# A hybrid decoder step on one core: in the Mamba stage, ScalarE and an adding transfer make every third block's second part, and ScalarE takes the convolution's first tap

## The chip, the cores and the metric

The kernel runs on one core of a Trainium2 chip. The metric is the device time of one execution in microseconds (us), smaller is better. The core's engines work side by side, each in the order of its own instructions: TensorE (PE in the rows; PEld is its loading of weights), VectorE (DVE), ScalarE (ACT), GpSimd (POOL) and SyncE (SP, which here only issues transfers). SBUF is the memory on the chip that they share; PSUM is the small memory into which TensorE writes.

## The reference

One inference step of a trunk of two layers, in fp32, for a prompt of 512 positions and a sample group of 8 x 8, which share the weights. The even layer is windowed attention beside an S5 state space model, the odd layer is a Mamba-2 mixer, and each is followed by an MLP. The change lies in the odd layer:

```python
def _mamba2(h, conv_buf, ssm_h0, w_in, conv_w, conv_b, dt_bias, a_log, d_skip, gnorm_w, w_out):
    zxbcdt = h @ w_in
    z, xbc, dt = ...
    xbc_full = jnp.concatenate([left, xbc], axis=1)
    conv = lax.conv_general_dilated(xbc_full, conv_w[:, None, :].astype(xbc.dtype), ...)   # 4 taps, causal, per channel
    xbc_c = jax.nn.silu(conv.astype(f32) + conv_b.astype(f32))
    x, bm, cm = ...
    dt = jax.nn.softplus(dt.astype(f32) + dt_bias.astype(f32)).reshape(bsz, l, G_C, J_C)
    y, h_last = _ssd(x * dt[..., None], dt * a, bm, cm, h0, chunk)
    ...
    g = (y * jax.nn.silu(z.astype(f32)))
    g = g * lax.rsqrt(jnp.mean(g * g, axis=-1, keepdims=True) + RMS_EPS)
    out = g.astype(h.dtype) @ w_out
```

## The kernel before

All 576 positions (512 + 64) lie along the free dimension, in two halves of 288 (`HV`), and the channels lie on the 128 partitions. A matrix product in fp32 is made of three products of parts: a weight block `w` of 128x1024 (8 pieces of 128x128) is split into a first part `wh`, which is `w` rounded to the form that TensorE multiplies, and a second part `wl` = `w` − `wh`; the activations are split in the same way into `xh` and `xl`. TensorE adds `wh`·`xh`, `wh`·`xl` and `wl`·`xh` (L326, L347 and L348 for the input projection, L1289 to L1291 for the output projection), over 8 pieces and two halves: 48 matmuls for a block.

`split_block` (L302) makes the parts. SP loads the raw block of 512 KB into a ring of two buffers (`NW` = 2). ScalarE copies it to `wh` (`copy_a`, L290). Then L312 subtracts on VectorE, or, for every third block (`SHARE_ODD` = 3, counted in `self.blocks`), on GpSimd. `wh` and `wl` have two buffers each in this stage. A raw buffer is free again, and the next load into it can start, when both parts have been made.

`odd` (L1108) is the Mamba stage, about 780 to 1345 us of the profiled execution. Its projection has 41 blocks: z (blocks 0 to 15), x (16 to 31), B (32 to 35), C (36 to 39) and dt (40). The blocks of x, B and C go through `raw_evac` (L1150ff), where ScalarE copies the result from PSUM to a tile `raw`, half by half, and GpSimd copies its last columns to `cvo`. Then `conv_tile` (L1138) follows: the first tap with the bias gives `cacc` on GpSimd (L1141), taps two to four are added on VectorE (L1143), ScalarE takes the tanh `cth` (L287), and VectorE multiplies it with `cacc` to x, B or C (L1146, L1148). There are 24 such tiles of 128x600. `dt_post` makes from dt what the state space scan needs, among it `tq` (L1238 to L1242 on VectorE), which TensorE transposes (L1247). `ssd_group` computes the scan for a group of heads, `gate` and `gated_norm` follow, then `out_proj`.

Two things set the order of work. The string `ODD_ORDER` gives the order in which the program names its parts: `s` a piece of the scan, `b`, `x` and `z` a part of the projection, `a`, `g` and `o` gate, norm and output projection. A scheduler then sets the order of instructions on each engine from that program and from modelled times; so an instruction that moves to another engine can move others too. An engine then runs its instructions strictly in that order.

Of the kernel before, what the change touches and what calls it, by code (L numbers as in the profile page):

```python
# [9 lines left out]
F32 = mybir.dt.float32  # L10
F32R = mybir.dt.float32r
ACTF = mybir.ActivationFunctionType
ALU = mybir.AluOpType
# [204 lines left out]
class _Kernel:  # L218
# [83 lines left out]
    def split_block(self, src, ring=None, cuts=1):  # L302

        raw = self.block(src, (8, 128), ring, cuts)
        hi, lo = self.part_tiles()
        self.blocks += 1
        eng = self.nc.gpsimd if self.share and self.blocks % self.share == 0 else self.nc.vector
        n = 8 // cuts
        for i in range(cuts):
            f = lambda t: t[:, i * n:i * n + n].rearrange("p a b -> p (a b)")  # L310
            self.copy_a(f(hi), f(raw))
            eng.tensor_tensor(f(lo), f(raw), f(hi).bitcast(F32), ALU.subtract)  # L312
        return hi, lo

    def pin(self, place):
# [796 lines left out]
    def odd(self, h, spill, done):  # L1112
        nc, tc, a = self.nc, self.tc, self.a
        tt, v = nc.vector.tensor_tensor, nc.vector
        stt = nc.vector.scalar_tensor_tensor
        with ExitStack() as es:
# [13 lines left out]
            cw = od.tile([128, 120], F32, name="cw")  # L1130
# [7 lines left out]
            def conv_tile(m, raw, out):  # L1138

                acc = od.tile([128, 600], F32, tag="cv", name=self.nm("cacc"), bufs=NCV)  # L1140
                nc.gpsimd.tensor_scalar(acc, raw[:, 0:600], cw[:, 4 * m:4 * m + 1], cw[:, 96 + m:97 + m], ALU.mult, ALU.add)  # L1141
                for k in range(1, 4):
                    stt(acc, raw[:, k:k + 600], cw[:, 4 * m + k:4 * m + k + 1], acc, op0=ALU.mult, op1=ALU.add)  # L1143
                th = od.tile([128, 600], F32, tag="cv", name=self.nm("cth"), bufs=NCV)
                self.act(th, acc, ACTF.Tanh)
                stt(out[:, 0:SEQ], th[:, 0:SEQ], 1.0, acc[:, 0:SEQ], op0=ALU.add, op1=ALU.mult)  # L1146
                s_in = lambda t: t[:, 512:600].rearrange("p (b k) -> p b k", b=8)[:, :, 3:11]
                stt(out[:, SEQ:].rearrange("p (b t) -> p b t", b=8), s_in(th), 1.0, s_in(acc), op0=ALU.add, op1=ALU.mult)  # L1148
# [19 lines left out]
            def evac(mt, hf, ps):  # L1168
                sl = slice(*HV[hf])
                if mt == 40:  # L1170

                    v.tensor_scalar(dtr[:, sl], ps[:96], po[:96, 696:697], None, ALU.add)
                    return
                if mt < 16:

                    if mt not in zs:
                        zs[mt] = ol.tile([128, T], F32, tag="z", name=self.nm("z"), bufs=4)
                    th = od.tile([128, HALF], F32, tag="cv", name=self.nm("zth"), bufs=NCV)
                    self.act(th, ps, ACTF.Tanh, scale=0.5)
                    stt(zs[mt][:, sl], th, 1.0, ps, op0=ALU.add, op1=ALU.mult)  # L1180
                    return
                m = mt - 16
                if not raw_evac(m, hf, ps):
                    return
                raw = raws.pop(m)
                if m < 16:
                    xs[m] = ol.tile([128, T], F32, tag="xs", name=self.nm("xs"), bufs=NXS)
                    conv_tile(m, raw, xs[m])
                else:
                    key = ("B" if m < 20 else "C", (m - 16) % 4)  # L1190
                    bc[key] = od.tile([128, T], F32, tag=key[0], name=self.nm(key[0]), bufs=2)
                    conv_tile(m, raw, bc[key])
# [78 lines left out]
            m = self.halves(self.mring)  # L1271
# [415 lines left out]
```

## Time and profile before

| | |
|---|---|
| median of 3 executions | 1770.38 us (1768.38 to 1774.1) |
| the profiled execution, its own time | 1776.06 us |
| its span, from the first instruction to the last | 1773.9 us |
| mean granted clock of TensorE | 0.967 of full speed |
| busy: TensorE | 1665.1 us (94%) |
| busy: VectorE | 1190.5 us (67%) |
| busy: ScalarE | 770.9 us (43%) |
| busy: GpSimd | 670.4 us (38%) |

The busy times are of one profiled execution and a mean over stages with different limits. A time in a row is counted from the start of the span. In a row, `wl<-w,wh` says that the instruction writes `wl` and reads `w` and `wh`; a releaser, as in `<-ACT wh L290`, is the work that ended last of what the instruction waited for.

### The profile page before, as it was taken

Reading aid. Unit: us, or ns where it says so; the run is one execution under the profiler, and the core shown is the slowest. Engines: PE = TensorE matmul, PEld = TensorE weight load, DVE = VectorE, ACT = ScalarE, POOL = GpSimd, SP = SyncE. Lnnn points to the kernel's source line nnn. Section 1 sums busy time; section 2 is a strip of 40 time slices with the busy share of each in tenths; the row PEclk is TensorE's granted clock in tenths of the full one; section 3 lists DMA queues with packets and bytes.
Section 4 is the critical chain, followed back from the end, with each engine's and each line's share of the span. In section 5 each row is a group of like instructions: output and inputs, shape, how many; then the busy total and the mean of one; then the engine's idle time right before and its main releaser. Section 6 shows DMA issues by size and latency. Waiting matters only on the chain.

```text
span 1773.9 us, 31866 instructions
## 1 busy us (share of the span) xinstructions
PE 1665.1 (94%) x12719; PEld 1532.1 (86%) x12719; DVE 1190.5 (67%) x2045; ACT 770.9 (43%) x1506; POOL 670.4 (38%) x705
## 2 busy tenths in 40 slices
PE   8998999899999999998799899999977999999997
PEld 8875565799999999997789789899857999999996
DVE  8656434467668676358788866977667866767634
ACT  5233433455554444334325536335245555344431
POOL 3533100245445362034365434442344644436102
PEclk9999899899999999999899999999978999999999
DMA  8568554530232313223142141241513033231311
GB/s 276 108 227 308 187 191 163 183 97 13 84 107 72 120 48 120 84 67 111 48 139 82 48 161 60 81 147 53 188 59 126 29 93 98 72 119 48 120 59 54
DMA packets 81652, 197.42 MB, mean 111 GB/s; under 512 B 20352, under 2 KB 32000, under 8 KB 81504
## 3 DMA queue, kind: packets, MB, share of 16 engines
q1 hardware_dynamic: 57568, 174.72, 29.8%
q10 hardware_dynamic: 23936, 20.67, 4.0%
q8 instruction: 100, 1.64, 0.4%
q14 instruction: 48, 0.39, 0.1%
HBM read 176.92 MB, written 18.44 MB: 110 GB/s over the span
## 4 chain that ended last, share of the span: by engine, by line
PE 38%; DVE 7%; ACT 2%; POOL 2%; issue 1%; DMA 1%; DVEq 0%; ACTq 0%; POOLq 0%
PE project L326 7%; PE project L347 7%; PE project L348 7%; PE pair L1100 2%; PE pair L1101 2%; PE pair L1102 2%; PE out_proj L1291 2%; PE out_proj L1289 2%; PE out_proj L1290 2%; PE ssd_group L1499 1%; DVE m L381 1%; DVE wl L312 1%; PE ssd_group L1420 1%; PE ssd_group L1454 1%; DVE cacc L1143 1%
## 5 line engine op out<-in xcount | busy, mean ns | idle before, releaser
L326 PE MATMUL project<-h,wh 128*128 128x288 f32 x1808 | 545.9, 303 | 26.8 <-ACT wh L290 9.7
L347 PE MATMUL project<-h,wh 128*128 128x288 f32 x1808 | 544.8, 302 | 7.0 <-DVE h L403 6.6
L348 PE MATMUL project<-h,wl 128*128 128x288 f32 x1808 | 542.0, 301 | 2.9 <-DVE wl L312 2.9
L326 PEld LDWEIGHTS project<-h,wh 128*128 128x128 f32 x1808 | 346.1, 192 | 38.9 <-ACT wh L290 11.7
L347 PEld LDWEIGHTS project<-h,wh 128*128 128x128 f32 x1808 | 347.1, 192 | 16.0 <-DVE h L403 9.2
L290 ACT ACTIVATE wh<-w 128x1024 fp32r<-128x1024 f32 (+1 forms) x239 | 216.6, 920 | 325.4 <-PE pair L1101 94.6
L348 PEld LDWEIGHTS project<-h,wl 128*128 128x128 f32 x1808 | 346.2, 192 | 10.0 <-issue 4.2
L312 DVE TENSOR_TENSOR wl<-w,wh 128x1024 fp32r<-128x1024 f32 (+1 forms) x148 | 189.3, 1285 | 104.1 <-ACT wh L290 101.6
L203 POOL TENSOR_TENSOR nacc<-nacc,nsq 128x288 f32<-128x288 f32 x88 | 83.1, 945 | 249.2 <-ACT nsq L287 235.6
L1014 POOL TENSOR_TENSOR a2t<-a2t,a2t 128x288 f32<-128x288 f32 x80 | 83.9, 1065 | 172.6 <-ACT a2t L287 167.8
L1101 PE MATMUL pair<-at,wh 128*128 128x288 f32 x384 | 112.8, 296 | 1.1 <-DVE at L355 1.1
L1102 PE MATMUL pair<-at,wl 128*128 128x288 f32 x384 | 111.7, 295 | 0.0
L1100 PE MATMUL pair<-at,wh 128*128 128x288 f32 x384 | 111.3, 295 | 0.0
L355 DVE TENSOR_TENSOR at<-a2t,at 128x288 fp32r<-128x288 f32 x96 | 65.8, 689 | 34.6 <-ACT at L290 34.6
L1067 DVE TENSOR_TENSOR wl<-ws,wh 128x512 fp32r<-128x512 f32 x96 | 83.0, 903 | 4.3 <-ACT wh L290 3.5
L1100 PE MATMUL pair<-a,wh 128*128 128x288 f32 x288 | 85.2, 296 | 0.6 <-DVE a2t L1006 0.6
L1101 PE MATMUL pair<-a,wh 128*128 128x288 f32 x288 | 84.8, 295 | 0.0
L1102 PE MATMUL pair<-a,wl 128*128 128x288 f32 x288 | 84.4, 295 | 0.5 <-DVE wl L1067 0.5
L1289 PE MATMUL out_proj<-x,wh 128*128 128x288 f32 x256 | 77.4, 304 | 3.0 <-DVE m L1296 2.5
L1143 DVE SCALAR_TENSOR_TENSOR cacc<-raw,cw,cacc 128x600 f32<-128x600 f32 x72 | 69.7, 968 | 13.5 <-POOL cacc L1141 12.5
L1291 PE MATMUL out_proj<-x,wl 128*128 128x288 f32 x256 | 76.9, 304 | 0.7 <-POOL wl L312 0.4
L1290 PE MATMUL out_proj<-x,wh 128*128 128x288 f32 x256 | 76.9, 301 | 0.0
(522 smaller groups left out, 3904.4 us busy)
## 6 DMA issues: line engine op xcount, KB each, us to landing
w<-in_w_dn SPq DMA_DIRECT2D x64, 512.0 KB, 3.5
w<-in_w_up SPq DMA_DIRECT2D x64, 512.0 KB, 3.5
w<-in_ck SPq DMA_DIRECT2D x40, 512.0 KB, 5.5
w<-in_cv SPq DMA_DIRECT2D x40, 512.0 KB, 5.8
w<-in_w_in_o SPq DMA_DIRECT2D x40, 512.0 KB, 3.5
w<-in_w_out_o SPq DMA_DIRECT2D x20, 512.0 KB, 3.5
hb<-in_h SPq DMA_DIRECT2D x32, 256.0 KB, 3.7
out_ssm_s<-hn ACTq DMA_DIRECT2D x32, 256.0 KB, 3.6
```

The costliest lines, as they stand in the source:

```text
L290: return self.nc.scalar.activation(out, in_, ACTF.Identity, **kw)
L312: eng.tensor_tensor(f(lo), f(raw), f(hi).bitcast(F32), ALU.subtract)
L326: self.nc.tensor.matmul(*args, **kw)
L347: self.nc.tensor.matmul(out, wh[:, c, :], xl, start=False, stop=False)
L348: self.nc.tensor.matmul(out, wl[:, c, :], xh, start=False, stop=(c == 7))
L1100: nc.tensor.matmul(ps, wh, xh, **(dict(start=True) if p in begin and c == 0 else go_on), stop=False)
L1101: nc.tensor.matmul(ps, wh, xl, **go_on, stop=False)
L1102: nc.tensor.matmul(ps, wl, xh, **go_on, stop=c == 3)
L1143: stt(acc, raw[:, k:k + 600], cw[:, 4 * m + k:4 * m + k + 1], acc, op0=ALU.mult, op1=ALU.add)
L1289: nc.tensor.matmul(out, wh[:, c, :], gh[:, k, :], start=(k == 0), stop=False)
L1290: nc.tensor.matmul(out, wh[:, c, :], gl[:, k, :], start=False, stop=False)
L1291: nc.tensor.matmul(out, wl[:, c, :], gh[:, k, :], start=False, stop=(k == 3))
```

## The change

It has two parts, both in the Mamba stage. For every third block, ScalarE writes −`w` into `wl`, in a second copy beside the one to `wh`, rounded to the same form, and then a transfer that GpSimd issues adds `w` to it in place (`accum_op`), from SBUF to SBUF, 512 KB each; GpSimd's subtraction falls away. And the first tap of the convolution, `raw` times a weight per channel plus a bias per channel, is a ScalarE instruction with two pointer operands where it was one of GpSimd. There are 19 such blocks and 24 such taps. Below L312 all lines of the changed kernel stand 5 higher.

```diff
@@ split_block
-        eng = self.nc.gpsimd if self.share and self.blocks % self.share == 0 else self.nc.vector
+        by_dma = self.share and self.blocks % self.share == 0
         n = 8 // cuts
         for i in range(cuts):
             f = lambda t: t[:, i * n:i * n + n].rearrange("p a b -> p (a b)")
             self.copy_a(f(hi), f(raw))
-            eng.tensor_tensor(f(lo), f(raw), f(hi).bitcast(F32), ALU.subtract)
+            if by_dma:
+
+                self.copy_a(f(lo), f(raw), scale=-1.0)
+                self.nc.gpsimd.dma_start(f(lo), f(raw), accum_op=ALU.add)
+            else:
+                self.nc.vector.tensor_tensor(f(lo), f(raw), f(hi).bitcast(F32), ALU.subtract)
@@ conv_tile
-                nc.gpsimd.tensor_scalar(acc, raw[:, 0:600], cw[:, 4 * m:4 * m + 1], cw[:, 96 + m:97 + m], ALU.mult, ALU.add)
+                self.copy_a(acc, raw[:, 0:600], scale=cw[:, 4 * m:4 * m + 1], bias=cw[:, 96 + m:97 + m])
                 for k in range(1, 4):
                     stt(acc, raw[:, k:k + 600], cw[:, 4 * m + k:4 * m + k + 1], acc, op0=ALU.mult, op1=ALU.add)
```

How the instructions stand now, at three places. The first is GpSimd's queue about `dt_post`, where x, B and C tiles go through the convolution (numbers behind the names tell tiles apart). Before:

```order
L1164 COPY cvo<-raw_8813 128x24
L1163 COPY cvo<-raw_8848 128x3
L1164 COPY cvo<-raw_8848 128x24
L1141 TENSOR_SCALAR cacc_8982<-raw_8813,cw 128x600
L1163 COPY cvo<-raw_8883 128x3
L1164 COPY cvo<-raw_8883 128x24
L1141 TENSOR_SCALAR cacc_9021<-raw_8848,cw 128x600
L312 TENSOR_TENSOR wl_9653<-w_9650,wh_9652 128x1024
L1345 COPY t_1284_9266<-tq_9248 96x256
L1345 COPY t_1295_9301<-B_8942 128x2x96
L1141 TENSOR_SCALAR cacc_9060<-raw_8883,cw 128x600
```

And now:

```order
L1168 COPY cvo<-raw_8849 128x3
L1169 COPY cvo<-raw_8849 128x24
L1168 COPY cvo<-raw_8884 128x3
L1169 COPY cvo<-raw_8884 128x24
L315 DMA wl_9654<-w_9651 128x1024
L1350 COPY t_1284_9267<-tq_9249 96x256
L1350 COPY t_1295_9302<-B_8943 128x2x96
```

The taps have gone, and where the subtraction stood there is the issue of a transfer, behind the same copies to `cvo` and ahead of the same copy of `tq`.

The second place is VectorE's queue at the same point, where `dt_post` ends in the product of `tq` with `dtr`, for which TensorE's transposes wait. Before:

```order
L1228 TENSOR_TENSOR stk<-acs_9239,stk 32x576
L1143 SCALAR_TENSOR_TENSOR cacc_9021<-raw_8848,cw,cacc_9021 128x600
L1146 SCALAR_TENSOR_TENSOR C_8981<-cth_8987,cacc_8982 128x512
L1148 SCALAR_TENSOR_TENSOR C_8981<-cth_8987,cacc_8982 128x64
L1241 TENSOR_TENSOR tq_9248<-tq_9248,dtr 32x576
```

And now:

```order
L1233 TENSOR_TENSOR stk<-acs_9240,stk 32x576
L1148 SCALAR_TENSOR_TENSOR cacc_8983<-raw_8814,cw,cacc_8983 128x600
L1246 TENSOR_TENSOR tq_9249<-tq_9249,dtr 32x576
L1151 SCALAR_TENSOR_TENSOR C_8982<-cth_8988,cacc_8983 128x512
L1153 SCALAR_TENSOR_TENSOR C_8982<-cth_8988,cacc_8983 128x64
```

The product with `dtr` stands ahead of the two pieces of C now, and a tap still stands ahead of both.

The third place is ScalarE's queue where the projection of the next group's x tiles begins, about 868 to 886 us of the profile before. Before:

```order
L290 ACTIVATE raw_9681<-project_1385_9685 128x224
L290 ACTIVATE raw_9681<-project_1385_9685 128x8x8
L290 ACTIVATE xws_9309<-xw_1302_9323 96x512
L290 ACTIVATE wh_9874<-w_9872 128x1024
L290 ACTIVATE xws_9309<-xw_1304_9332 96x512
L287 ACT_TABLE_LOAD
L287 ACTIVATE cth_9720<-cacc_9715 128x600
L290 ACTIVATE raw_9755<-project_1392_9730 128x288
```

And now:

```order
L290 ACTIVATE raw_9683<-project_1385_9687 128x224
L290 ACTIVATE raw_9683<-project_1385_9687 128x8x8
L290 ACTIVATE cacc_9717<-raw_9683,cw 128x600
L290 ACTIVATE xws_9310<-xw_1302_9324 96x512
L290 ACTIVATE xws_9310<-xw_1304_9333 96x512
L290 ACTIVATE wh_9876<-w_9874 128x1024
L290 ACTIVATE wl_9877<-w_9874 128x1024
L287 ACT_TABLE_LOAD
L287 ACTIVATE cth_9722<-cacc_9717 128x600
L290 ACTIVATE raw_9757<-project_1392_9732 128x288
```

The first tap comes right behind the evacuation that feeds it, and between it and the evacuation of the next tile there is one copy more, −`w` into `wl`.

## Rows read from the trace of the kernel before

**Rows 1.** Stretches: length, busy time (instructions) of each engine, granted clock, DMA share, GB/s.
```profile
core 0: us, PE busy (x) PEld busy (x) DVE busy (x) ACT busy (x) POOL busy (x), PEclk, DMA share, GB/s
740.00:780.00 40.00, 40.00 (x298) 39.73 (x296) 14.33 (x28) 8.09 (x20) 11.03 (x13) 1.00 0.17 48
...
820.00:860.00 40.00, 32.01 (x206) 29.59 (x205) 34.76 (x52) 14.55 (x29) 21.05 (x24) 0.83 0.20 66
```

**Rows 2.** TensorE's waits, 780 to 1345 us: us in total, times, longest.
```profile
PE project L326 <- ACT raw L290: 9.2, 4, 4.0
```

**Rows 3.** Timeline of TensorE: start, us, instruction [idle before it <- what ended it].
```profile
846.16 0.58 PE L1247 MATMUL dt_post<-ident,tq 96*128 96x96 f32 x2 [6.31 <-DVE tq L1241]
...
1011.06 0.56 PE L326 MATMUL project<-h,wh 128*128 128x288 f32 x1 [3.41 <-ACT raw L290]
```

**Rows 4.** Stretches behind the two holes, columns as in rows 1.
```profile
843.90:857.50 13.60, 9.66 (x36) 7.48 (x37) 11.45 (x21) 3.40 (x9) 5.90 (x12) 0.50 0.03 10
...
1011.20:1014.50 3.30, 3.30 (x14) 3.30 (x15) 2.33 (x4) 0.17 (x2) 1.77 (x4) 0.50 0.00 0
```

**Rows 5.** GpSimd's groups by form, 780 to 1345 us: busy, mean ns | idle before.
```profile
L312 POOL TENSOR_TENSOR wl<-w,wh 128x1024 fp32r<-128x1024 f32 x19 | 48.4, 2549 | 57.5 <-ACT wh L290 53.2 <-DVE mt L1487 4.3
...
L1141 POOL TENSOR_SCALAR cacc<-raw,cw 128x600 f32<-128x600 f32 x24 | 29.4, 1223 | 1.7 <-DVE cacc L1143 1.7
```

**Rows 6.** Timeline of VectorE before the holes at 846 and 880.
```profile
839.21 2.37 DVE L1239 TENSOR_TENSOR tq<-acs 32x64 f32<-32x64 f32 x1
841.60 0.45 DVE L1242 TENSOR_SCALAR tq<-acs 32x576 f32<-32x576 f32 x1
...
844.51 0.68 DVE L1146 SCALAR_TENSOR_TENSOR C<-cth,cacc 128x512 f32<-128x512 f32 x1
...
875.44 2.84 DVE L1143 SCALAR_TENSOR_TENSOR cacc<-raw,cw,cacc 128x600 f32<-128x600 f32 x1
```

**Rows 7.** Timeline of GpSimd: four of the subtractions and one first tap.
```profile
838.75 2.74 POOL L312 TENSOR_TENSOR wl<-w,wh 128x1024 fp32r<-128x1024 f32 x1
...
987.93 2.41 POOL L312 TENSOR_TENSOR wl<-w,wh 128x1024 fp32r<-128x1024 f32 x1 [7.90 <-ACT wh L290]
...
991.14 3.71 POOL L1141 TENSOR_SCALAR cacc<-raw,cw 128x600 f32<-128x600 f32 x1
...
1266.09 2.37 POOL L312 TENSOR_TENSOR wl<-w,wh 128x1024 fp32r<-128x1024 f32 x1 [3.90 <-ACT wh L290]
...
1333.13 2.40 POOL L312 TENSOR_TENSOR wl<-w,wh 128x1024 fp32r<-128x1024 f32 x1
```

**Rows 8.** The tile `cacc`: ns min/median/max, first and last start.
```profile
L1143 DVE SCALAR_TENSOR_TENSOR cacc<-raw,cw,cacc x72: 824/844/2839, 827.2 to 1145.9; 128x600 f32<-128x600 f32 x72
L1141 POOL TENSOR_SCALAR cacc<-raw,cw x24: 836/842/4145, 826.3 to 1141.9; 128x600 f32<-128x600 f32 x24
```

**Rows 9.** Timeline of ScalarE before the hole at 880.
```profile
878.36 1.28 ACT L287 ACT_TABLE_LOAD   x1 [2.88 <-DVE cacc L1143]
```

**Rows 10.** ScalarE's groups by form, 780 to 1345 us, columns as in rows 5.
```profile
L290 ACT ACTIVATE wh<-w 128x1024 fp32r<-128x1024 f32 x63 | 66.2, 1055 | 96.7 <-PE project L347 42.6 <-issue 21.3 <-PE out_proj L1290 19.6
...
L287 ACT ACTIVATE cth<-cacc 128x600 f32<-128x600 f32 x24 | 16.8, 701 | 45.9 <-DVE cacc L1143 45.9
```

**Rows 11.** ScalarE's copies at L290, whole span, columns as in rows 8.
```profile
L290 ACT ACTIVATE raw<-project x72: 211/348/412, 799.2 to 1141.2; 128x288 f32<-128x288 f32 x24, 128x224 f32<-128x224 f32 x24, 128x64 f32<-128x64 f32 x24
L290 ACT ACTIVATE h<-x,normw x32: 517/521/539, 3.4 to 407.2; 128x288 fp32r<-128x288 f32 x32
...
L290 ACT ACTIVATE x<-xs x32: 428/435/447, 983.7 to 1319.1; 128x288 fp32r<-128x288 f32 x32
```

**Rows 12.** Issues of transfers: count, KB each, median us from issue to landing.
```profile
w<-in_w_in_o SPq DMA_DIRECT2D x40, 512.0 KB, 3.5
...
u<-ud ACTq DMA_DIRECT2D x8, 144.0 KB, 7.2
```

**Rows 13.** Timeline of TensorE: first products with a second part from GpSimd.
```profile
993.33 0.29 PE L348 MATMUL project<-h,wl 128*128 128x288 f32 x1
...
1275.42 0.29 PE L1291 MATMUL out_proj<-x,wl 128*128 128x288 f32 x1
```

## Prediction

> **What bounds the kernel now.** I read the busy time by stretches first. Where nothing is missing TensorE is full: 40.00 of 40 us from 740 to 780; in the Mamba stage, 820 to 860, it works 32.01 us at a mean granted clock of 0.83, while VectorE works 34.76 of the 40 [rows 1]. So TensorE sets the time and what can be won are its holes. Next I read what TensorE waits for in the stage (780 to 1345 us). The largest item that touches the change is ScalarE's evacuation of the projection to `raw`: 9.2 us in four waits, the longest 4.0 [rows 2], the one that ends at 880.7. Then I looked up the holes one by one: 6.31 us before 846.16, where the transposes of `dt_post` wait for VectorE's `tq`, and 3.41 us before 1011.06, again for `raw` [rows 3]. Behind both, the granted clock is at the lower of its two levels (0.50 of 2.4 GHz, so 1.2 GHz): for 13.6 us from 843.9, for 3.3 us from 1011.2 [rows 4]. What GpSimd gives up is 19 subtractions of 2.55 us and 24 first taps of 1.22 us, 78 us in all [rows 5]; that is no gain by itself, since GpSimd is not the bound. Only what its work holds up counts.
>
> **Gains.** (1) *Hole before 846.* VectorE's piece of `tq` on 32x64 takes 2.37 us, the one behind it, nine times as wide, 0.45 [rows 6]. It overlaps GpSimd's subtraction of 838.75 to 841.49 [rows 7]: VectorE is held by it. Without that subtraction I give the piece 0.3 us, which wins 2.1. In the new order VectorE multiplies `tq` by `dtr` before it writes C, and C's first piece alone is 0.68 us [rows 6]; with its second I take 0.9. Together −3.0.
>
> (2) *Hole before 880.7.* VectorE's last tap at 875.44 takes 2.84 us against a median of 0.84 [rows 6, 8], under the subtraction that falls there. ScalarE waits 2.88 us for that tap, loads a table (1.28 us), does the tanh and only then evacuates [rows 9]. Freed, this tap would come 2.0 us earlier; but ScalarE now has its second copy in the same place, 1.06 us, of which I charge 0.8. So −1.2.
>
> (3) *Hole before 1011.* GpSimd's first tap at 991.14 takes 3.71 us, the median is 0.84 [rows 7, 8]; the taps behind it on VectorE and, through the tanh, two evacuations to `raw` follow that chain. On ScalarE the tap stands right behind the evacuation that feeds it. Its price there: the tanh of 128x600 takes 0.701 us [rows 10]; a 128x288 copy with a pointer operand takes 0.521 us against 0.435 without [rows 11], so 0.79 for one pointer and 0.87 for two; I take 0.8. That wins 2.9, and with the hole nearly shut the 3.3 us at half clock behind it should go too, which are worth half of them, 1.7. Together −4.6.
>
> Sum of gains: 3.0 + 1.2 + 4.6 = 8.8 us. The third hole's 4.6 and the 2.1 of the first are the bounds' soft spots: each could be nothing if the next thing on the engine is late instead.
>
> **Losses.** (4) *The transfer's latency.* A subtraction gives the second part about 2.4 us after the first. Now ScalarE writes −raw (1.06 us, as the 1.055 of the 63 first parts [rows 10]), and a transfer X follows from GpSimd's queue. The trace has no transfer from that queue, none inside SBUF and none that adds. Bounds from rows: 3.5 us, a plain load of the same 512 KB, and 7.2 us, the slowest of the small forms [rows 12]. (A transfer without price is excluded: it moves as many bytes as the load.) I take 3.5 us and a second reading of the same bytes: 48 GB/s at a share of 0.17 [rows 1] make 282 GB/s at full share, 512 KB in 1.9 us; X = 5.4, so the part comes 1.06 + 5.4 − 2.4 = 4.1 us later than now.
>
> What hides that is the time between the end of GpSimd's subtraction and the first product that needs it. I read it for the 16 blocks between 838 and 1277 us: 18.5, 9.4, 6.3, 4.3, 5.1, 3.0, 4.1, 5.2, 6.6, 4.7, 5.6, 7.0, 5.9, 4.7, 6.3, 7.0. The tightest ends at 990.34 and is used at 993.33; the last ends at 1268.46 and is used at 1275.42 [rows 7, 13]. At 4.1 us later only the tightest waits: +1.1. At X = 6.5 the stalls sum to 5.1, at 7.2 to 10, at 8 to 18. The block at the stage's head has no such cover; its delay mostly falls into waits that follow it anyway, so I charge +0.5.
>
> On the page "DMA: Bandwidth & Descriptors" (Anatomy of one DMA, GpSimd's path) the Trainium skill gives a fixed 2.0 us and 436 GB/s; from it I estimate 3.2 us for 512 KB, 4.4 with two readings. By that the stalls would be under 0.3 us and the sum lower by one. No run here shows it.
>
> (5) *ScalarE's queue.* It gets 19 x 1.06 + 24 x 0.8 = 39 us more in 565, and it works in order. A `raw` evacuation (72 pieces [rows 11]) meets one of the new instructions in 39/565 = 7% of cases and waits half of one, 0.5 us: 72 x 0.07 x 0.5 = 2.5 us if PSUM's buffers hide nothing, 0 if they hide all; I take +1.5. Behind the new copies also stand first parts of other blocks and the tanh.
>
> (6) *The tail.* The last of the blocks is on the path of the output projection: 1333.13, 2.40 us [rows 7], used as soon as it is there. Later by up to 4.1 us; against that GpSimd, which does the sums of squares there, is free of 2.4 us of subtraction ahead of them. Bounds −2.4 to +4.1, taken +1.0.
>
> (7) At nothing: GpSimd's issue of 19 transfers. It waits there for ScalarE's −raw, and behind it stand copies to `cvo` and GpSimd's own sums, none of which TensorE waits for soon; cover gone, it is what (6) bounds. VectorE and SP keep their counts; but `w` comes free only when the transfer has landed, 4.1 us later, and SP's next load waits for that. With a block in about 9 us (63 in 565 us [rows 10]) and two raw buffers, a load of 3.5 us still fits.
>
> **Sum.** −8.8 + 1.1 + 0.5 + 1.5 + 1.0 = −4.7 us. The profiled execution took 1776.06 us (its span 1773.9), so 1771.4; it lies 5.7 us above the median of 1770.38, and against that the forecast is **1765.7**. The measurement of this kernel can tell about 0.3%, 5.3 us, from no change; the forecast is close to that edge.
>
> **Rivals.** *A: the transfer is slow, and it is slower than before.* The trace shows GpSimd's work held by VectorE: its first tap took up to 4.145 us instead of 0.842 [rows 8]. If issuing a transfer is held like that, 5.4 plus most of 3.3 us gives X = 8, stalls of 18 us instead of 1.1, and −8.8 + 18 + 0.5 + 1.5 + 1.0 = +12, 1782.6. It decides from X = 7.4 (stalls of 11) on. Against it: half of the blocks have 5.5 us or more of cover, and not every issue would meet a long VectorE instruction. The page "SBUF — State Buffer" of the Trainium skill (Summary: rules for kernel authors) has this as a rule: GpSimd's writing of descriptors is starved while VectorE runs in a mode with two ports, and such transfers are better issued from another engine. The trace agrees as far as GpSimd's compute is held; no run here shows an issue held. Chance 0.27.
>
> *B: nothing comes of it, since ScalarE takes the place of GpSimd.* Gains (2) and (3) need ScalarE at once, and it has table loads and copies in line there [rows 9]. Without them −3.0 + 4.1 = +1.1, 1771.5. For it: in the stretch of 880 ScalarE was what TensorE waited for; against it: it works 14.55 of 40 us from 820 to 860 [rows 1]. Chance 0.20.
>
> *C: more comes of it.* If the hole before 846 shrinks so far that the 13.6 us at half clock [rows 4] do not follow, up to (857.5 − 846.2)/2 = 5.7 us are won on top: 1760. For it: the hole halves; against it: 3 us remain, and a hole of 3.41 was followed by half clock as well. Chance 0.13.
>
> **Numbers.** The forecast's own case has 0.40, and its range is 1762 to 1770 (X of 3.5 to 6.5 and ScalarE's 0 to 2.5); nearly half of it lies beyond 0.3%. Faster: all of C, 0.19 of the forecast, 0.04 of B: 0.36. Same: 0.18 of the forecast, 0.12 of B, 0.03 of A: 0.33. Slower: 0.24 of A, 0.04 of B, 0.03 of the forecast: 0.31. The range to leave out 2 in 10 runs from 1757, beyond C, to 1783, just past A.
>
> **What would show it.** Transfers from GpSimd's queue: landing 5.4 us after issue, or 8 and more. Waits of TensorE in the products with `wl` for a transfer: about 1 us in all, not 10. VectorE's `tq` pieces all under 0.5 us and no tap of 2.8 us; the hole before `dt_post` near 3.3 us. No hole for `raw` above 1 us about 1011 and no half clock behind it; ScalarE's copies with `cw` at 0.8 us. Wrong it would be above all if many parts arrive after TensorE has come to them, or if the waits for `raw` stay with ScalarE as the last to come.

## The result, and the profile after

The changed kernel took 1762.58 us (median of 8 runs, 1759.7 to 1767.71) beside 1770.94 us for the kernel before (8 runs, 1758.38 to 1781.79): a ratio of 0.9947 with a 95% interval of 0.9924 to 0.997. Measured a second time it gave 0.9978 (0.9954 to 1.0001). Both together say some 4 to 9 us faster, though the interval of the second reaches 1.0001, so that it alone does not tell the change from none; the forecast of 1765.7 us, 4.7 us faster, lies at the lower end.

Two spans can't be compared as they are. The profiled execution of before has a span of 1773.9 us, that of after 1757.9 us. But half of these 16 us arise in the even layer, which neither part of the change touches: the Mamba stage's early matmuls come 8 us earlier already. TensorE's order there is the same in both, and that layer differs from one execution to the next: 500 of its matmuls take 57.1 us in one profile of before and 63.5 in another. So I compare stretches with the same work: from TensorE's n-th matmul to its m-th, which in both kernels are 12719 matmuls in all. The table gives microseconds, worked out from the start times of the matmuls in each profile; 6000 is just ahead of the stage, 10250 in the MLP behind it. The order of TensorE differs a little between the kernels: up to the 8500th a boundary parts the same matmuls but for four at most (13 with the double transfer), at 9500 and behind it exactly the same. At 9250 twelve matmuls of the output projection have come ahead of the boundary in the change and twelve of the scan behind it, so 8500 to 9500 is best read as one: 136.4 us before, 142.0 and 141.7 with the change. The kernels below the fourth line are the experiments that follow.

```
from matmul             6000   6250   6500   6750   8500   9250   9500   9750
to                      6250   6500   6750   8500   9250   9500   9750  10250   sum
before                  43.3   46.0   40.7  244.7   98.2   38.2   49.4   90.0  650.5
before, again           43.4   45.9   40.7  244.7   98.2   38.2   49.3   90.1  650.5
the change              44.2   44.6   35.9  236.8   98.4   43.6   54.9   84.5  642.9
the change, again       47.0   44.8   35.9  240.5   98.1   43.6   52.5   86.3  648.7
transfer alone          45.8   44.5   39.0  243.3   98.3   44.0   53.8   86.0  654.7
tap alone               48.8   48.3   34.9  240.1  104.1   41.5   47.9   89.5  655.2
tap, all on VectorE     46.6   47.5   34.8  240.5   99.1   41.1   48.8   86.8  645.2
double transfer         47.4   44.7   36.9  246.2  108.8   34.8   58.8   88.2  665.9
last group VectorE      46.6   44.8   35.9  237.5   98.3   43.6   48.3   87.4  642.3
last group GpSimd       46.1   44.7   35.9  236.8   98.2   43.6   47.4   89.1  641.7
projection only         44.1   44.5   35.9  239.8   99.3   43.3   46.9   86.5  640.2
other third             48.7   46.1   35.3  238.5   98.2   41.5   51.6   85.1  645.0
every second            44.9   44.0   40.3  236.4   97.2   40.9   47.1   86.2  637.0
projection GpSimd       43.6   48.3   34.9  242.6   99.2   41.1   48.0   87.6  645.4
```

The reader is to see three things. The kernel before repeats itself to 0.1 us in every stretch (its two profiles are of executions of nearly the same time, 1776.06 and 1776.27 us), the change differs by 5.8 us between two profiles (of executions of 1759.7 and 1767.86 us). The change wins 10 to 14 us from 6250 to 8500. And it gives 8.5 to 11 us back from 9250 to 9750, of which 4 to 5.5 return behind it.

The stretch in which most is won, in the view by stretches (the columns of rows 1; from the 6500th matmul to the 8500th), of before:

```profile
870.40:1155.80 285.40, 269.66 (x2003) 245.82 (x2001) 221.60 (x333) 127.26 (x236) 135.98 (x165) 0.98 0.29 96
```

and after:

```profile
861.80:1134.60 272.80, 265.16 (x2003) 241.29 (x2002) 207.60 (x328) 150.35 (x264) 105.12 (x145) 1.00 0.38 116
```

The same 2003 matmuls take 12.6 us less. VectorE, which lost no instruction of its own to the change (five of 333 have left this stretch), works 14.0 us less, ScalarE 23 us more, GpSimd 31 us less, and no half clock is left in this profile's stretch. What TensorE waits for in the stage after the change (us in total, times, longest), which answers to [rows 2, 3]:

```profile
PE ssd_group L1504 <- POOL mt L1492: 5.7, 2, 3.6
PE project L331 <- ACT wh L290: 5.2, 4, 1.7
PE project L331 <- ACT raw L290: 4.7, 5, 1.5
...
PE out_proj L1296 <- DMA wl<-w: 2.7, 2, 1.6
PE project L353 <- DMA wl<-w: 2.6, 3, 1.7
...
PE ssd_group L1486 <- ACT ce__1996_13429 L287: 2.4, 1, 2.4
PE dt_post L1252 <- DVE tq L1246: 2.2, 1, 2.2
```

The waits for `raw` fell from 9.2 to 4.7 us, the one for `tq` from 6.3 to 2.2. In their place stand 5.3 us of waits for transfers, 2.2 us more for first parts from ScalarE, and a new one for `ce`.

VectorE's queue ahead of `dt_post`, the place of [rows 6], in the timeline of after:

```profile
830.76 0.21 DVE L1244 TENSOR_TENSOR tq<-acs 32x64 f32<-32x64 f32 x1
830.99 0.45 DVE L1247 TENSOR_SCALAR tq<-acs 32x576 f32<-32x576 f32 x1
...
833.20 0.84 DVE L1148 SCALAR_TENSOR_TENSOR cacc<-raw,cw,cacc 128x600 f32<-128x600 f32 x1
834.08 0.75 DVE L1246 TENSOR_TENSOR tq<-tq,dtr 32x576 f32<-32x576 f32 x1
834.88 0.69 DVE L1151 SCALAR_TENSOR_TENSOR C<-cth,cacc 128x512 f32<-128x512 f32 x1
```

The piece of 2.37 us takes 0.21, and C stands behind the product. The tiles of `cacc` (columns as in rows 8):

```profile
L1148 DVE SCALAR_TENSOR_TENSOR cacc<-raw,cw,cacc x72: 823/843/1760, 820.0 to 1121.9; 128x600 f32<-128x600 f32 x72
L290 ACT ACTIVATE cacc<-raw,cw x24: 872/889/893, 819.0 to 1117.9; 128x600 f32<-128x600 f32 x24
```

No tap of 2.8 us is left; ScalarE's tap takes 0.889 us. And the transfers, from the view of their line, issue on GpSimd (ns min/median/max) and landing:

```profile
L315 POOL DMA_DIRECT2D wl<-w x19: 852/878/1039, 783.7 to 1320.5; - x19
...
DMA to landing us min/median/max: 4.5/4.7/6.7
```

### The profile page after: what moved, and what is told of

The parts are those of the page before. It is cut to its first block, busy times and chain, and to the rows that moved or that the text cites. A ratio compares the mean times of both kernels' runs of the same rounds, so it can differ in the third digit from the quotient of the medians.

```text
span 1757.9 us, 31900 instructions
## 1 busy us (share of the span) xinstructions
PE 1658.0 (94%) x12719; PEld 1523.5 (87%) x12719; DVE 1176.7 (67%) x2045; ACT 807.9 (46%) x1549; POOL 615.9 (35%) x681
## 4 chain that ended last, share of the span: by engine, by line
PE 74%; DVE 13%; ACT 6%; DMA 4%; issue 2%; POOL 1%; SPq 0%; ACTq 0%; DVEq 0%; POOLq 0%
PE project L331 14%; PE project L353 14%; PE project L352 14%; PE pair L1105 5%; PE pair L1106 5%; PE pair L1107 5%; DVE wl L317 2%; PE out_proj L1296 2%; PE out_proj L1294 2%; PE out_proj L1295 2%; DVE m L386 2%; PE s L928 1%; PE ssd_group L1504 1%; ACT wh L290 1%; ACT L287 1%
## 5 line engine op out<-in xcount | busy, mean ns | idle before, releaser
L331 PEld LDWEIGHTS project<-h,wh 128*128 128x128 f32 x1808 | 341.9, 189 | 31.8 <-ACT wh L290 12.0
L290 ACT ACTIVATE wh<-w 128x1024 fp32r<-128x1024 f32 (+1 forms) x239 | 216.7, 920 | 311.1 <-PE pair L1106 94.5
L353 PEld LDWEIGHTS project<-h,wl 128*128 128x128 f32 x1808 | 342.3, 190 | 17.2 <-issue 6.7
L352 PEld LDWEIGHTS project<-h,wh 128*128 128x128 f32 x1808 | 342.9, 190 | 12.1 <-DVE h L408 5.7
L331 PE MATMUL project<-x,wh 128*128 128x288 f32 x256 | 76.6, 299 | 5.0 <-DVE m L1011 5.0
```

The source lines that it names most:

```text
L290: return self.nc.scalar.activation(out, in_, ACTF.Identity, **kw)
L331: self.nc.tensor.matmul(*args, **kw)
L352: self.nc.tensor.matmul(out, wh[:, c, :], xl, start=False, stop=False)
L353: self.nc.tensor.matmul(out, wl[:, c, :], xh, start=False, stop=(c == 7))
```

## The experiments

Theory 1 is that of the prediction: GpSimd's work holds VectorE, each part of the change frees a part of it, and the gains of the parts add up. The rivals: that the tap alone does it and the transfer costs what it wins (theory 2), and that the order of instructions does it, by accident.

**Only the transfer.** From the changed kernel:

```diff
-                self.copy_a(acc, raw[:, 0:600], scale=cw[:, 4 * m:4 * m + 1], bias=cw[:, 96 + m:97 + m])
+                nc.gpsimd.tensor_scalar(acc, raw[:, 0:600], cw[:, 4 * m:4 * m + 1], cw[:, 96 + m:97 + m], ALU.mult, ALU.add)
```

> Only the first part of the change: second parts of every third block by ScalarE and the adding transfer; the first tap stays on GpSimd. Theory 1 (the subtraction on GpSimd holds VectorE and its absence wins the holes at 846 and 880; the tap on ScalarE wins the one at 1011): 3 to 6 us faster than before, the hole ahead of dt_post at 2 to 3 us, holes for raw about 1000 stay at 3 us. Theory 2 (the gain is the tap's alone, the transfer costs in waits for wl what it wins): within 2 us of before or slower, waits of TensorE for transfers of about 5 us.

Measured: 1.0003 (0.9987 to 1.002), no gain in total, as theory 2 had it; the waits for transfers are 4.5 us. What it frees is seen: the pieces of `tq` are short again. But two holes stay, in TensorE's timeline:

```profile
848.10 0.42 PE L1252 MATMUL dt_post<-ident,tq 96*128 96x96 f32 x1 [5.19 <-DVE tq L1246]
...
880.25 0.40 PE L331 MATMUL project<-h,wh 128*128 128x288 f32 x1 [2.14 <-ACT raw L290]
```

and the waits of the stage say why:

```profile
POOL wl L315 <- ACT wl L290: 41.2, 9, 9.9
...
DVE cacc L1148 <- POOL cacc L1146: 16.5, 16, 2.2
...
PE project L331 <- ACT raw L290: 9.2, 7, 2.3
```

VectorE waits 16.5 us for first taps, where it waited 12.5 before; GpSimd has its queue held up by issues that wait for ScalarE's −`w`, and the taps stand in that queue too. The waits for `raw` are 9.2 us, as before. By the table this kernel still wins 4.6 us from 6250 to 8500; it loses 10.2 us from 9250 to 9750, as the change does, of which 4.0 return behind it. So its total does not say that the transfer wins nothing where the holes are.

**Only the tap.** From the kernel before:

```diff
-                nc.gpsimd.tensor_scalar(acc, raw[:, 0:600], cw[:, 4 * m:4 * m + 1], cw[:, 96 + m:97 + m], ALU.mult, ALU.add)
+                self.copy_a(acc, raw[:, 0:600], scale=cw[:, 4 * m:4 * m + 1], bias=cw[:, 96 + m:97 + m])
```

> Only the second part: first tap on ScalarE; GpSimd keeps its subtractions. Theory 1: 3 to 5 us faster than before, no waits for transfers, VectorE's pieces under a subtraction still reach 2 us and more, the hole ahead of dt_post stays near 6 us. Theory 2: as fast as the whole change or faster, 8 us and more below before.

Measured: 0.9995 (0.9977 to 1.0013), no gain either, so both theories missed. By the table it has the tap's gain, 5.8 us from 6500 to 6750 and 4.6 from there to 8500, and loses 7.8 us up to 6500 and 5.9 from 8500 to 9250. One of these losses is the subtraction, still there. GpSimd's timeline at that place:

```profile
839.21 2.45 POOL L312 TENSOR_TENSOR wl<-w,wh 128x1024 fp32r<-128x1024 f32 x1 [6.27 <-ACT wh L290]
```

and VectorE's:

```profile
839.19 0.21 DVE L1239 TENSOR_TENSOR tq<-acs 32x64 f32<-32x64 f32 x1
839.43 2.54 DVE L1242 TENSOR_SCALAR tq<-acs 32x576 f32<-32x576 f32 x1
```

The subtraction came half a microsecond later against VectorE's queue than in [rows 6, 7] and holds the next piece: the same 2 us, another victim. The Trainium skill has this as a rule on the page "SBUF — State Buffer" (Who interferes with whom): for some kinds of VectorE instruction the two engines share a pair of ports, and whoever comes second stands still until the other's instruction is over. The rows agree: GpSimd is done at 841.66, and VectorE's piece at 841.97.

The loss from 8500 to 9250 is the same thing in another place. On GpSimd, on VectorE and then on TensorE:

```profile
1231.10 2.40 POOL L312 TENSOR_TENSOR wl<-w,wh 128x1024 fp32r<-128x1024 f32 x1 [0.86 <-ACT wh L290]
...
1231.21 2.60 DVE L355 TENSOR_TENSOR x<-xs,x 128x288 fp32r<-128x288 f32 x1
...
1235.16 1.19 PE L1420 MATMUL ssd_group<-xw,btk 128*128 128x512 f32 x1 [3.52 <-DVE xw L1417]
```

The median of these pieces of `x` is 0.450 us; behind this one stands `xw`, for which TensorE waits 3.52 us, and then the granted clock is 0.50 from 1235.0 to 1240.5. The loss up to 6250 I did not trace; that stretch differs by 2.8 us between the two profiles of the change.

**The tap, and all second parts on VectorE.** From the changed kernel, so that neither GpSimd nor a transfer is left:

```diff
-SHARE_ODD = 3
+SHARE_ODD = 0
```

> First tap on ScalarE; no block is shared, VectorE makes all second parts. Theory 1: VectorE gets 19 x 1.2 = 23 us more and is the engine that is waited for about 820 to 900 and 980 to 1020, so 3 to 8 us slower than the whole change, though no part comes late through a transfer (waits for transfers 0). Theory 2: the transfers are what costs, so at least as fast as the whole change.

Measured: 0.9962 (0.994 to 0.9985), 645.2 us in the stage. Theory 1 said 3 to 8 us slower than the change, and that is not borne out: 0.9962 lies between the change's 0.9947 and 0.9978, and the intervals overlap. Theory 2 is borne out so far that the transfer, as the change places it, buys little over VectorE. From 6500 to 8500 it takes 275.3 us, as the kernel with the tap alone. What the transfers win over it lies in 6250 to 6500, 44.6 against 47.5 us.

**A second transfer ahead of each.** From the changed kernel; ahead of each adding transfer a transfer copies the tile onto itself, which changes no value:

```diff
+                self.nc.gpsimd.dma_start(f(lo), f(lo))
                 self.nc.gpsimd.dma_start(f(lo), f(raw), accum_op=ALU.add)
```

> The whole change with the latency of the transfer about doubled: ahead of the adding transfer stands one that copies the second part onto itself, so a part comes 4 to 6 us later and GpSimd issues 38 transfers. Theory 1, with the cover read from the kernel before (3 to 18.5 us a block): at 4.5 us more, X of 9.2, the stalls sum to 30 us less what the order hides, so 10 to 30 us slower than the whole change and waits of TensorE for transfers of 15 to 35 us. A rival, that the time is set elsewhere and transfers are hidden anyway: under 5 us slower.

Measured: 1.0072 (1.0044 to 1.01). Against 0.9947 this is 1.0126, 22 us slower than the change (17 us against 0.9978), inside what theory 1 gave; the longer transfers are not hidden. But the waits put down to transfers are 13.6 us, less than the 15 to 35 expected. Its transfers, KB and us to landing:

```profile
wl<-wl POOLq DMA_DIRECT2D x19, 512.0 KB, 3.0
...
wl<-w POOLq DMA_DIRECT2D x19, 512.0 KB, 5.0
```

and the waits:

```profile
PE project L354 <- DMA wl<-w: 6.9, 5, 2.2
...
PE out_proj L1297 <- DMA wl<-w: 6.7, 4, 2.9
```

The adding transfer is issued 3.4 to 5.7 us behind the plain one (median 4.1), since GpSimd's queue first waits for that to land, 27.3 us in 11 waits. So the edit does two things: a part comes some 4 us later, and GpSimd's other work stands behind the wait. Together they cost 8.3 us more of waits for transfers and 17 to 23 us in the stage; that a late part costs more than its own wait is likely, but not parted here from GpSimd's own delay. In that profile half clock goes with the longest of these waits (2.91 us before 1253.14, and 0.50 from 1252.3 to 1259.1); how the rest divides I did not take apart.

**The last output projection without transfers.** Two of the 19 blocks, to VectorE or to GpSimd's subtraction:

```diff
+                    self.share = SHARE_ODD if g + 1 < G_C else 0
                     out_proj(g, gn.pop(g), both if g + 1 < G_C else by_half)
```

> The whole change, but the two shared blocks of the last output projection (group 3) get their second part from VectorE, without a transfer; 17 transfers remain. In the profile of the change TensorE needs 98.5 us from its 9250th to its 9750th matmul, where the kernel before needs 87.6 and the kernel without transfers (all second parts on VectorE) 89.9. Theory 1, the transfers near the end delay the last blocks, since no other work covers them there: 88 to 92 us in this stretch and 4 to 9 us faster than the whole change. Rival, the order of the instructions about the last pieces of the scan costs it: the stretch stays above 95 us and the time within 2 us of the whole change.

Measured: 0.9945 (0.9928 to 0.9963).

```diff
+                    self.last_g = g + 1 == G_C
                     out_proj(g, gn.pop(g), both if g + 1 < G_C else by_half)
...
-            if by_dma:
+            if by_dma and getattr(self, "last_g", False):
+                self.nc.gpsimd.tensor_tensor(f(lo), f(raw), f(hi).bitcast(F32), ALU.subtract)
+            elif by_dma:
```

> The whole change, but the two shared blocks of the last output projection go to GpSimd's subtraction as before the change. Theory 1 (no cover for a transfer near the end): as with VectorE there, 88 to 92 us from the 9250th to the 9750th matmul, 3 to 8 us faster than the whole change; GpSimd's sums of squares start 2.4 us later, so up to 3 us slower than with VectorE. Rival (order): above 95 us, no faster than the whole change.

Measured: 0.9954 (0.9937 to 0.9972). The table splits the matter in two. From 9500 to 9750 the loss is gone: 48.3 and 47.4 us, against 54.9 and 52.5 of the change and 49.4 of before. So two late transfers cost 4 to 7.5 us there, as theory 1 had it. From 9250 to 9500 nothing moved, 43.6 us in both; these transfers are not its cause, and the rival, the order, is left for it. And behind 9750 the two kernels lose 1 to 5 us, which the change had not lost, so the stage takes 642.3 and 641.7 us, and the change 642.9 and 648.7. The sums of both stretches, 91.9 and 91.0 us, lie at the upper edge of the 88 to 92 that theory 1 gave; the total that it gave, 3 to 9 us faster than the change, came against the second measurement of the change (4 to 6 us) and not against the first.

**Transfers in the input projection alone.** From the changed kernel; all parts for the four output projections on VectorE, 13 transfers left:

```diff
+                    self.share = 0
                     out_proj(g, gn.pop(g), both if g + 1 < G_C else by_half)
+                    self.share = SHARE_ODD
```

> The whole change, but every block of the four output projections gets its second part from VectorE; 13 transfers remain, all in the input projection. Theory 1: as the kernel with VectorE for the last group alone, and no wait of 1.65 us for the transfer of the third group; 5 to 10 us faster than the whole change. Rival, VectorE is short in the third group too: no faster than that kernel, 2 us slower.

Measured: 0.9921 (0.9904 to 0.9938). It is faster than the change by 0.26% against its first measurement, by 0.57% against its second; 5 to 10 us were expected, 4.6 to 10 came. Only the second of these differences has intervals that do not overlap. Against the kernel with the tap and all second parts on VectorE (0.9962, 0.994 to 0.9985) it is 0.4% faster, and the intervals just do not touch: here the transfers do buy something over VectorE.

**Another third of the blocks.** From the changed kernel:

```diff
-        by_dma = self.share and self.blocks % self.share == 0
+        by_dma = self.share and self.blocks % self.share == 1
```

> The whole change with the same kinds and nearly the same numbers of instructions, but the blocks taken are those whose count leaves 1 on division by 3, not 0, so that transfers fall in other places. If the gain comes from what GpSimd gives up (theory 1): within 4 us of the whole change, and the stretch from the 6500th to the 8500th matmul at 240 to 244 us as in the change (before 252.9). If the gain is an accident of the order: 5 us and more slower, and that stretch near 250.

Measured: 0.9942 (0.9921 to 0.9963), as the change; 273.8 us from 6500 to 8500, where the change took 272.7 and 276.4 and before 285.4. (The 240 to 244 and 252.9 in the expectation were added up wrongly, without the stretch from 6750 to 7000.) The gain does not hang on which blocks are taken, so it is no accident of one order. For the transfers that stretch is no test, since the tap alone takes 275.1 us there; the total is.

**Three kernels on one chip: the change again, every second block, GpSimd in the projection.** The second and third start from the kernel with transfers in the projection alone:

```diff
-SHARE_ODD = 3
+SHARE_ODD = 2
```

```diff
-                self.copy_a(f(lo), f(raw), scale=-1.0)
-                self.nc.gpsimd.dma_start(f(lo), f(raw), accum_op=ALU.add)
+                self.nc.gpsimd.tensor_tensor(f(lo), f(raw), f(hi).bitcast(F32), ALU.subtract)
```

> The changed kernel itself, a second time, on the same chip and beside the same runs of the kernel before as the two that follow: for their comparison, and for how much one profile differs from the next. Both theories: 0.993 to 0.997 of before; 640 to 646 us from the 6000th to the 10250th matmul.

> As the kernel with transfers in the input projection alone, but every second block in place of every third, 19 transfers in place of 13. If VectorE's time is what is still short in the projection: 2 to 5 us faster than with every third. If the cover of the transfers is used up, or ScalarE (6 more copies of 1.05 us), 2 to 8 us slower, with more waits for transfers than the 2.6 us there.

> As the kernel with transfers in the input projection alone, but the 13 blocks go to GpSimd's subtraction in place of copy and transfer; the tap stays on ScalarE, the output projection's parts on VectorE. Theory 1 (a subtraction on GpSimd holds VectorE): 4 to 12 us slower than with transfers, VectorE's time above its medians 10 us and more higher in the projection. Rival (what matters is only that the output projection has no shared blocks): within 2 us of it.

Measured: the change 0.9978 (0.9954 to 1.0001) at 1767.52 us, every second block 0.9927 (0.9904 to 0.9951) at 1759.36 us, GpSimd in the projection 0.9968 (0.9941 to 0.9994) at 1767.58 us. The change itself missed what both theories gave it (0.993 to 0.997, and 640 to 646 us in the stage, which took 648.7). Every second block is as good as every third, and neither of the two things expected of it came: it is not measurably faster or slower, and its waits for transfers are 1.4 us, not above 2.6; its 12 runs (1754.0 to 1762.47) all lie below the 12 of the change (1764.32 to 1771.8). With GpSimd's subtractions back in the projection VectorE's work from 6500 to 8500 is 218.85 us:

```profile
863.70:1141.20 277.50, 266.91 (x2003) 244.30 (x2001) 218.85 (x328) 141.96 (x253) 119.94 (x145) 0.99 0.29 94
```

against 210.01 us with the transfers in the projection alone:

```profile
865.30:1141.00 275.70, 268.33 (x2002) 244.44 (x2001) 210.01 (x329) 148.98 (x262) 104.43 (x144) 0.99 0.38 112
```

The expectation spoke of time above the medians. I took every instruction of VectorE from the 6000th to the 8500th matmul against the median of its like in ten of these profiles: the sum above the medians is 28 us here and 17 us with the transfers, 11 more, where 10 and more were expected. It is 29 us before, 25 with the tap alone moved, 22 with the subtractions alone moved, 15 and 16 with the change, and 12 where neither subtraction nor tap nor transfer is left on GpSimd. So both kinds of work hold VectorE. And the old waits are back:

```profile
PE project L329 <- ACT raw L290: 7.7, 4, 3.4
PE dt_post L1250 <- DVE tq L1244: 4.2, 1, 4.2
```

Against the kernel with transfers it is 0.5% slower, about 8 us (the same 8 us against every second block, on the same chip), as theory 1 had it.

**The kernel before, profiled again.**

> The kernel before, profiled a second time, to see which of its holes come back: theories of this study need the hole of 6 us ahead of dt_post, the ones of about 4 and 3.4 us for raw and half clock behind them in this profile too, and 647 to 654 us from the 6000th to the 10250th matmul. If they were accidents of one execution, the holes are smaller and the stretch is below 645.

Measured: the same holes (6.29, 4.04 and 3.41 us, where [rows 2, 3] have 6.31, 4.0 and 3.41), half clock in the same places, 650.5 us in the stage. Rows of the kernel before were no accident.

## Why the prediction was right, and where it was not

The sign (in the second measurement only just), the size (4.7 us forecast, 9.4 and 3.9 by the two ratios) and the mechanism held. The steps behind them held unequally.

(1) *Hole before 846*: right in the row, too high in time. The hole shrank by 4.1 us, more than the 3.0 charged, but the stretch that holds it only by 1.2 to 1.4. Part of what TensorE no longer waits there it waits a little later, 1.46 us for `raw` at 845.93, and the half clock behind the hole stayed, for 13.7 us:

```profile
836.20:849.90 13.70, 10.52 (x37) 7.80 (x37) 11.83 (x21) 5.35 (x12) 2.95 (x8) 0.50 0.11 38
```

That also decides rival C: a hole of 2.18 us did not spare it. What the transfer does there is plain, though: with the tap on ScalarE the stretch takes 47.5 us when VectorE makes the second parts, 48.3 when GpSimd does, and 44.0 to 44.8 with transfers (46.1 with the other third).

(2) *Hole before 880.7*: mis-sized and put down to the wrong part. Charged with −1.2, it gave −4.8. The tap alone gave 5.8, the transfer alone 1.7. The chain to ScalarE's evacuation was read rightly; that the first tap on GpSimd was a link of that chain as well I had not seen. (With every second block the stretch takes 40.3 us again, though the tap is on ScalarE; why is open.)

(3) *Hole before 1011*: right in size, and once more in the next group, which I had not counted. From the 7000th to the 7500th matmul the change won 5.1 and 3.5 us (73.7 to 68.6 and 70.2) against the 4.6 charged; it is not the tap's alone, since the transfer alone won 2.7 there (71.0) and the tap alone 3.2 (70.5); half clock behind 1011 was gone in the first profile and back in the second, for 3.4 us from 988.8. From 8000 to 8500, in the next group, it won another 4.2 and 2.7 (75.3 to 71.1 and 72.6). The tap's price was 0.889 us, not 0.8: two pointers, as the upper of the two estimates had it.

*The sum of (1) to (3)*, in which the gains of both parts are added, held where these holes lie: from 6250 to 8500 the transfer alone wins 4.6 us, the tap alone 8.1, both 14.1 and 10.2, against 8.8 charged. In VectorE's own queue the parts add up as well (29 us above the medians, 25 and 22 with one of them, 15 and 16 with both). What I had not seen is that each part alone gains nothing in total (1.0003 and 0.9995). Outside these stretches the transfer alone loses 8.8 us and the tap alone 12.8, both together 6.5 and 8.4. For the transfer that is mostly the tail; for the tap it is in part the subtraction that is left, which holds VectorE at another place. It need not do so everywhere: with the tap moved and 13 subtractions left, all in the projection, the kernel ran at 0.9968. Of each part alone there is one profile, so differences of a few us between them are not sure.

(4) *The transfer*: X was 4.7 us, not 5.4. By the list of covers that X would have stalled TensorE for 0.4 us; there were 2.6 us of waits in the projection, where 1.6 was charged, and 2.7 more in the output projection. So X was taken too long and the cover too long as well. The tightest block did wait, as said, 1.67 us:

```profile
981.82 0.40 PE L353 MATMUL project<-h,wl 128*128 128x288 f32 x1 [1.67 <-DMA wl<-w]
...
1224.37 0.40 PE L1296 MATMUL out_proj<-x,wl 128*128 128x288 f32 x1 [1.65 <-DMA wl<-w]
```

The second was not foreseen. Its issue waited for ScalarE until 1218.93, where the first part was begun at 1215.91: between the two copies on ScalarE now stood an `x` and a `zth`, and the cover I had read belonged to the old order. The Trainium skill's figures ("DMA: Bandwidth & Descriptors", Anatomy of one DMA) gave an estimate of 3.2 us, or 4.4 with two readings; the 4.7 measured differ from both, and lie nearer to two readings.

(6) *The tail*: the term that failed in size. Charged with +1.0 and at most +4.1, the stretch from 9250 to 9750 cost 10.9 and 8.5 us, of which 5.5 and 3.7 came back behind it. Two late transfers were 4 to 7.5 us of it. The other 5.4, from 9250 to 9500 (38.2 to 43.6), is the same in every kernel that takes the change's thirds by transfer once, whatever the last group does (43.3 to 44.0 us); it is 40.9 and 41.5 where other blocks are taken and 41.1 to 41.5 without transfers. There TensorE waits for `ce` from ScalarE, 2.4 us before 1266.53, with half clock from 1266.3 to 1273.1. In the kernels with 43.3 to 44.0 us twelve matmuls of the output projection have changed places with twelve of the scan across the 9250th, in the others with a single transfer or none at most six; so TensorE's own order goes with this loss. But the kernels without transfers lose some 3 us here as well, and what in the order brings it about stays open; no kernel here takes it alone.

(5), *ScalarE's queue*, +1.5: of the right size as far as it can be read, 2.2 us more of waits for first parts, though not of the evacuations for which it was charged. Rival A did not come: all issues took 0.85 to 1.04 us, and the landings 4.5 to 6.7. What the page "SBUF — State Buffer" of the Trainium skill says (Summary: rules for kernel authors), that VectorE in its faster modes starves GpSimd's writing of descriptors, did not show in a stretch in which VectorE works 207.60 of 272.80 us; in which mode its instructions ran no run shows. The doubled transfer, 13 us slower than before at a part some 4 us later, fits rival A's price (+12 for X of 8). Rival B did not come: ScalarE stayed the one waited for, but for 4.7 us in place of 9.2.

So the good size of the forecast is in part luck, from two errors that cancel: gains that were larger (10.2 to 14.1 us net from 6250 to 8500, where 8.8 at most was charged; the surplus lies in 2 and in the group after 3), and losses that were dearer (6.5 to 8.4 us in all other stretches, where 4.1 at most was charged; the tail above all).

## What to carry to other kernels

An engine that is not the bound can still set the bound's pace. If VectorE and GpSimd work on SBUF side by side, look for instructions of VectorE that take far longer than their like, and see whether GpSimd's work spans them; here moving either kind of work off GpSimd alone brought nothing in total, and both together 0.2 to 0.5%. Use a transfer as an engine only where there is other work to cover its time (4.7 us here), and plain arithmetic where the program runs dry: here the transfers paid in the input projection, and in the output projection no gain from them shows, and the version that keeps them there alone ran at 0.9921 of before; its sister with every second block, on one chip with the change, took 0.9927 against the change's 0.9978. And read cover from the order that the change will have, not from the old one.

## What the runs showed that I had not expected

A transfer inside SBUF that adds 512 KB landed 4.7 us after its issue (4.5 to 6.7, in the second profile of the change up to 7.1), a plain one of the tile onto itself after 3.0; GpSimd was busy 0.88 us with issuing the first and 0.60 with the second. The kernel before repeated its stage to 0.1 us from one profile to the next, while the change differed by 5.8 us between two; that the 19 transfers bring this about is not shown.
